# One load for each unit's weights: sixteen shared 4 KB buffers in a hybrid attention layer

## The chip, the cores and the metric

The kernel runs on one core of a Trainium2 chip. The metric is the device time of one execution in microseconds (us); the median of several runs is compared. A core has TensorE (matrix products, PE in the profile, its weight loads PEld), VectorE (DVE), ScalarE (ACT), GpSimd (POOL) and SyncE (SP); in this kernel SyncE issues every transfer (DMA), one after the other from one queue. Working memory is SBUF, 128 partitions wide; a "4 KB buffer" has 4 KB in each partition, 512 KB in all. Sums of products are built up in PSUM.

## The reference

One layer of a streaming encoder runs over a prompt of 2048 rows and a sample of 8 x 16 rows with caches of 512 past positions. The width is 1024. Cut to what matters:

```python
def adaln_modulate(x, c, norm_g, w_ada, b_ada):
    shift, scale, gate = jnp.split(c @ w_ada + b_ada, 3, axis=-1)
    h = rms_norm(x, norm_g) * (1.0 + scale[:, None, :]) + shift[:, None, :]
    return h, gate[:, None, :]

def project_inputs(h, w_in, pos):
    # columns of w_in: 4 x 512 (branch A), 4 x 512 (branch B), 2 x 1024 (gates)
    qa, ka, va, za, qb, kb, vb, zb, ga, gb = jnp.split(h @ w_in, idx, axis=-1)
    ...  # rope on qa, ka

def diff_attention(q, k, v, qpos, kpos, lam):          # branch A, 4 heads
    p = softmax(where(mask, q @ k.T / 8, -inf))         # two maps a head
    return (p[0] - lam * p[1]) @ v

def stick_breaking_attention(q, k, v, qpos, kpos):     # branch B, 8 heads
    z = q @ k.T / 8
    log_1m = where(mask, log_sigmoid(-z), 0.0)
    log_a = log_sigmoid(z) + cumsum(log_1m, reverse=True) - log_1m
    return where(mask, exp(log_a), 0.0) @ v

def merge_branches(oa, ob, za, zb, ga, gb, ...):
    ya = (rms_norm(oa, subln_g) * (1 - lam_init) * silu(za)) @ w_branch_a
    yb = (ob * silu(zb)) @ w_branch_b
    return (sigmoid(ga) * ya + sigmoid(gb) * yb) @ w_out

y = rms_norm(x + gate * merge_branches(...), final_g)   # also returns the new keys and values
```

All inputs are fp32.

## The kernel before, in words

Every product in fp32 is made of fp16 products. An operand is scaled by a power of two and split into a high and a low fp16 part, and three products (high x high, high x low, low x high) are summed. The power of two depends on the operand's sum of squares. So a weight is touched twice: first a *norm* (a sum of squares on ScalarE, `sum_squares`, whose unused output is the tile `junk`), then, when all chunks of the operand have been summed and the scale is known, a *cut* (`split`, L266: the high part on ScalarE or GpSimd in turn, the low part on VectorE).

The work is in eight *units*, `u` from 0 to 7. Unit u takes head group `h = u // 2` of branch A (`u` even) or of branch B (`u` odd). A unit's projection weights are 512 columns of `w_in` (query, key, value and z of that head group), in four chunks of 256 rows; a chunk is one 4 KB buffer, loaded by two DMAs of 256 KB (L298). Units 1 to 6 also project 256 columns of the gates (two chunks of 512 KB, L309), unit 7 projects 512 (four chunks).

Each unit goes over 17 row tiles, the sample tile first (`t == NT`), then the 16 prompt tiles. `project` (L388) multiplies a tile of activations `hg`, fetched from memory one tile ahead (`fetch_h`, L384, three buffers), with the unit's weights `U["w"]` (24 products of 128 x 512 at L409) and the gate weights `U["wg"]` (24 products at L476); `finish` scales the result, splits it and stores keys, values and z. `scores` forms the attention scores of a tile (L611 to L615) and turns the weights by a transposing DMA (`turn`, L552, tile `wt`); `pv` multiplies them with the values (L659 to L664) two steps later.

The main loop (L1170) goes over the 136 steps `(u, t)`. At each step it lays side by side the score work of that step, the values' work of two steps before, and a part of the list of projection pieces, which runs about five tiles ahead of the scores (`LEAD`). At the first step of unit u the pieces of `prepare_unit(u + 1)` are put on the list `back` and are handed out over the first nine steps (`W_READY`). When that list is empty, the step takes from `spare`, the norms of the output weights and of the caches (`norms`, L801): 80 loads of 512 KB, each followed by one sum of squares. The order on each engine's queue is then set by a scheduler with a timing model of its own; it keeps to the data dependencies, and an instruction that needs a buffer again waits for the last user of it.

`prepare_unit` (L286) makes the pieces: four norms, `bounds` (the scale), then two cuts, then the norms and cuts of the gates. The other two cuts (chunks 4 and 6) are returned apart and kept in `late`; `begin` (L824) runs them when the unit's own projection starts. A norm loads its chunk into one of two buffers of the pool `wst`, and a cut loads it again into one of them. Cut weights lie in 12 buffers of 2 KB (`wpr`, tile `wpair`; a unit needs 8) and, for the gates, in six of 4 KB (`gwp`, tile `gw`, opened when the startup is over). The spare norms use the two `wst` buffers too. Unit 0 is different: its raw chunks lie in a large tile of the startup (`keep`) and are loaded once.

The startup (the `p0` pool) computes the modulation, prepares unit 0, norms, modulates and transposes x, and starts the first projections. After the last projection all pools of `proj` are closed, and their place is taken by the pools for the branch weights, the merge and the output; the sample's attention over the caches runs there too.

Of the kernel before, what the change touches and what calls it, by code (L numbers as in the profile page):

```python
# [16 lines left out]
F32 = mybir.dt.float32  # L17
F16 = mybir.dt.float16
# [7 lines left out]
P = 128  # L26
D = 1024
KT = D // P
# [13 lines left out]
SC_BUFS = 6  # L42
V_LO, V_HI = 0.1, 1.0
W_READY = 9
W_BUFS = 12
WIDE_BUFS = 6
P0_AT = 2.0, 4.0, 6.0
K_BUFS = 6
V_BUFS = 23
G_BUFS = 6  # L50
S_TILES = 13
S_PERIOD = 6
H_AT = 2
# [58 lines left out]
def layer_kernel(ctx: ExitStack, tc: tile.TileContext, a: dict):  # L112
# [61 lines left out]
    unit = ctx.enter_context(tc.tile_pool(name="unit", bufs=2))  # L174
    proj = ctx.enter_context(ExitStack())
    c01 = ctx.enter_context(ExitStack())
    wpr = proj.enter_context(tc.tile_pool(name="wpr", bufs=W_BUFS, side="right", reuse_waits="tile"))
    wst = proj.enter_context(tc.tile_pool(name="wst", bufs=2, side="right", reuse_waits="tile"))
    kvp = c01.enter_context(tc.tile_pool(name="kvp", bufs=2))
    stg = c01.enter_context(tc.tile_pool(name="stg", bufs=2))  # L180

# [64 lines left out]
    def sum_squares(src, n, dst, width=1024):  # L246

        for i in range(0, n, width):
            junk = tiny.tile([P, width], F16, tag="junk", name="junk", bufs=1)
            w = min(width, n - i)  # L250
            S.activation(out=junk[:, 0:w], in_=src[:, i : i + w], func=AF.Square,  # L251
                         accum_out=dst[:, i // width : i // width + 1])
# [32 lines left out]

    def prepare_unit(u, keep=None):  # L286

        kept = {}
        h, kind = u // 2, u % 2
        U = dict(h=h, kind=kind, u=u)  # L290
        units[u] = U

        def chunk(k):
            if k in kept:
                return kept[k]
            st = wst.tile([P, 2, 4, P], F32, tag="wst", name="wst") if keep is None else keep[:, k // 2, :, :, :]
            for i in range(2):
                load(out=st[:, i, :, :], in_=w_in[:, k + i, :].rearrange("p (j n) -> p j n", n=512)[:, 4 * kind : 4 * kind + 4, h * P : (h + 1) * P])  # L298
            st = st.rearrange("p k j n -> p k (j n)")
            if keep is not None:  # L300
                kept[k] = st
            return st

        g0, gw = GATES[u]
        gk = 1024 // gw if gw else 0

        def gate_chunk(k):
            st = wst.tile([P, 2, 4, P], F32, tag="wst", name="wst").rearrange("p a j n -> p (a j n)").rearrange("p (k n) -> p k n", k=gk)
            load(out=st, in_=w_in[:, k : k + gk, 4096 + g0 : 4096 + g0 + gw])  # L309
            return st  # L310

        def gate_norm(k):
            if k == 0:
                U["gacc"] = unit.tile([P, 4], F32, tag="gacc", name="gacc")
            sum_squares(gate_chunk(k).rearrange("p k n -> p (k n)"), 1024, U["gacc"][:, k // gk : k // gk + 1])

        def gate_cut(k):
            if k == 0:
                U["sg"] = scales(total(add_up(U["gacc"], KT // gk)), unit, "sg")
                U["wg"] = []  # L320
            st = gate_chunk(k)
            w = gwp.tile([P, gk, 2, gw], F16, tag="gw", name="gw", bufs=G_BUFS)
            split(w[:, :, 0, :], w[:, :, 1, :], st, U["sg"][:, 0:1], S if k else G)
            U["wg"].append(w)

        def norm(k):
            if k == 0:
                U["acc"] = unit.tile([P, 4], F32, tag="wacc", name="wacc")
            sum_squares(chunk(k).rearrange("p k n -> p (k n)"), 1024, U["acc"][:, k // 2 : k // 2 + 1])

        def bounds():
            fsq = total(add_up(U["acc"], 4))
# [3 lines left out]
            U["w"] = []  # L336

        def cut(k):
            st = chunk(k)
            for i in range(2):  # L340
                w = wpr.tile([P, 2, 512], F16, tag="wpair", name="wpair")
                split(w[:, 0, :], w[:, 1, :], st[:, i, :], U["sw"][:, 0:1], S if i % 2 else G)
                U["w"].append(w)

        early = [lambda k=k: norm(k) for k in range(0, KT, 2)] + [bounds] + [lambda k=k: cut(k) for k in (0, 2)]
        if gw:
            early += [lambda k=k: gate_norm(k) for k in range(0, KT, gk)] + [lambda k=k: gate_cut(k) for k in range(0, KT, gk)]
        return early, [lambda k=k: cut(k) for k in (4, 6)]

    def finish_unit(u):  # L350

# [36 lines left out]
    def project(U, t):  # L388
# [80 lines left out]
        def gate_piece(n):  # L469

            if n == 0:
                box["g"] = bank("t")
            for j in range(per * n, per * n + per):
                hi, wi = ((0, 0), (0, 1), (1, 0))[j % 3]
                k = j // 3
                T.matmul(box["g"][:, 0:gw], box["h"][:, hi, k, :], U["wg"][k // per][:, k % per, wi, :], start=(j == 0), stop=(j == 3 * KT - 1))  # L476
            if per * n + per == 3 * KT:
                gt = gwp.tile([P, 512], F32, tag="gt", name="gt", bufs=2)
# [322 lines left out]
    def norms():  # L801

        srcs = [w[:, k, :] for w in (w_ba, w_bb) for k in range(4)] + [w_out[:, k, :] for k in range(KT)]
        srcs = [(src, wsums[:, i : i + 1]) for i, src in enumerate(srcs)]
        srcs += [(caches[name][:, i * 8 : i * 8 + 8, h * P : (h + 1) * P], csums[:, cache_column(name, h), i : i + 1])
                 for name in caches for h in range(4) for i in range(4)]

        def one(src, dst):
            st = wst.tile([P, 2, 4, P], F32, tag="wst", name="wst").rearrange("p k j n -> p (k j n)")
            load(out=st if len(src.shape) == 2 else st.rearrange("p (j n) -> p j n", n=P), in_=src)  # L810
            sum_squares(st, 1024, dst)

        return [lambda src=src, dst=dst: one(src, dst) for src, dst in srcs]
# [4 lines left out]
    jobs = []  # L818


    late = {}
    line = []

    def begin(u, t):  # L824
        if t == NT:
            for fn in late.pop(u, []):
                fn()
            finish_unit(u)

    def projection(m):  # L830
# [44 lines left out]
    with tc.tile_pool(name="p0", bufs=1) as p0:  # L875
# [57 lines left out]
        xs = {}  # L933
        for n in range(3):
            modulation(n)
        early, late0 = prepare_unit(0, hp_tile(F32).rearrange("p (a k j n) -> p a k j n", k=2, j=4, n=P))
        for fn in early[0:4]:
            fn()
        modulation(3)
        for fn in early[4:] + late0:  # L940
            fn()
        xs[4] = load_x(16, 1)
        xs[0] = load_x(0, 4)
# [404 lines left out]
```

## Time and profile before

| | |
|---|---|
| median of 3 runs | 2494.43 us (2491.0 to 2498.75) |
| the profiled execution | 2503.67 us, its span 2501.9 us |
| mean granted TensorE clock | 0.94 of full speed |
| PE busy | 2162.8 us (86%) |
| DVE busy | 1807.2 us (72%) |
| ACT busy | 1602.2 us (64%) |
| POOL busy | 833.8 us (33%) |
| bytes moved by DMA | 477.07 MB |
| weight loads into `wst` | 112 of 256 KB and 32 of 512 KB |

The profile is one execution. A group of instructions is named by line, engine, operation and tiles, written `out<-in` with buffer numbers left out. A line of the waits reads: engine, tile and line that stood idle, what ended that idle time, microseconds in all, times, the longest. The chain of waits is followed back from the last instruction, at each step to what released it; a piece of it is shown with its start, its length and its name. In the list of DMAs the last figure is the median time from issue to landing. Instructions that only wait or issue a DMA do not count as busy. The matmuls' ends are modelled, so a busy PE is not a PE at its peak.

### The profile page before, as it was taken

The page shows a single profiled execution, that of the slowest core. Times are in us where ns is not written, and L with a number is a line of the kernel's source. Part 1 is how long each engine was busy: PE and PEld are TensorE (multiplying, and loading weights), DVE is VectorE, ACT ScalarE, POOL GpSimd, SP SyncE. Part 2 cuts the span into 40 slices and gives each one's busy share as a digit, 9 for nine tenths or more (in the row PEclk, how much of TensorE's full clock was granted, in tenths as well). Part 3 has the DMA queues.
Part 4 walks back from the last instruction along what each step waited for, and adds up shares of the span by engine and source line. Part 5 has one row for each costly group of instructions (what it writes and reads, how often), then busy time and mean ns, then how long its engine had stood idle before and what let it go on. Part 6 is the DMA issues. An engine that isn't in the chain of part 4 may idle for free.

```text
span 2501.9 us, 45310 instructions
## 1 busy us (share of the span) xinstructions
PE 2162.8 (86%) x16366; PEld 1263.7 (51%) x16366; DVE 1807.2 (72%) x3769; ACT 1602.2 (64%) x3200; POOL 833.8 (33%) x671
## 2 busy tenths in 40 slices
PE   4779898889989988899989889999975789888887
PEld 2445465545655555556555555555543344444443
DVE  4868657876665788667668866656787888787855
ACT  4658667876766778666677866656775545454442
POOL 1822023352101335321124532102353465443422
PEclk7989999999999999999999999999986889899999
DMA  8779778996777899777688976656678998997521
GB/s 304 270 184 215 183 185 202 207 209 158 187 204 170 202 206 223 169 158 184 165 201 190 217 178 168 168 134 141 146 170 214 270 232 238 225 237 209 155 97 52
DMA packets 890994, 477.07 MB, mean 191 GB/s; under 512 B 540074, under 2 KB 842330, under 8 KB 890256
## 3 DMA queue, kind: packets, MB, share of 16 engines
q1 hardware_dynamic: 890768, 474.17, 76.2%
q8 instruction: 128, 2.10, 0.4%
q14 instruction: 98, 0.80, 0.1%
HBM read 272.94 MB, written 73.44 MB: 138 GB/s over the span
## 4 chain that ended last, share of the span: by engine, by line
PE 40%; DMA 19%; DVE 16%; ACT 9%; issue 8%; POOL 4%; SPq 3%; DVEq 0%; POOLq 0%; ACTq 0%
PE ps_mm L409 16%; PE ps_t L476 9%; DMA hg<-hT_d 5%; DMA wt<-sc_n 4%; DMA wst<-in_w_in_dram 3%; DVE sc_n L588 3%; PE ps_s L611 2%; PE ps_mm L1235 2%; PE ps_s L612 2%; ACT junk L251 2%; ACT sc_p L121 2%; PE ps_o L1274 2%; DVE sc_n L545 1%; ACT ps_s L121 1%; DVE o L1127 1%
## 5 line engine op out<-in xcount | busy, mean ns | idle before, releaser
L409 PE MATMUL ps_mm<-wpair,hg 128*128 128x512 f16 x3120 | 790.1, 388 | 58.5 <-DMA hg<-hT_d 54.8
L594 POOL TENSOR_TENSOR sc_p<-sc_p,sc_n 128x127 f32<-128x127 f32 (+7 forms) x192 | 313.5, 1637 | 808.5 <-DVE sc_n L588 790.8
L409 PEld LDWEIGHTS <-hg 128*128 128x128 f16 x3120 | 279.2, 99 | 330.7 <-DMA hg<-hT_d 67.2
L476 PE MATMUL ps_t<-gw,hg 128*128 128x256 f16 (+1 forms) x2856 | 393.8, 292 | 2.5 <-DVE qst L504 1.7
L476 PEld LDWEIGHTS <-hg 128*128 128x128 f16 x2856 | 278.7, 99 | 96.3 <-DVE qst L504 2.5
L588 DVE TENSOR_TENSOR_SCAN sc_n<-ps_s,sc_n,zero_t 128x512 f32<-128x512 f32 x192 | 245.6, 1279 | 69.2 <-ACT ps_s L121 64.5
L611 PE MATMUL ps_s<-k,qst 128*128 128x512 f16 (+3 forms) x640 | 228.1, 358 | 52.4 <-DVE sc_n L588 41.3
L545 DVE TENSOR_TENSOR sc_n<-sc_p,sc_n 128x128 f16<-128x128 f32 (+7 forms) x192 | 234.5, 1227 | 36.8 <-ACT sc_n L544 36.2
L121 ACT ACTIVATE sc_p<-ps_s,usc 128x512 f32<-128x512 f32 (+3 forms) x320 | 204.8, 640 | 48.7 <-PE ps_s L612 24.0
L612 PE MATMUL ps_s<-k,qst 128*128 128x512 f16 (+3 forms) x640 | 227.6, 358 | 0.0
L1235 PE MATMUL ps_mm<-wb,uT 128*128 128x512 f16 x816 | 200.0, 398 | 21.4 <-DVE o L1133 13.0
L121 ACT ACTIVATE ps_s<-ps_s,usc 128x512 f32<-128x512 f32 (+3 forms) x328 | 199.8, 609 | 0.0
L1274 PE MATMUL ps_o<-wo,yT 128*128 128x512 f16 x816 | 193.8, 392 | 6.7 <-POOL wo L271 4.8
L663 PE MATMUL ps_o<-v,wt 128*128 128x128 f16 x1088 | 162.3, 228 | 42.4 <-DMA wt<-sc_n 42.4
L544 ACT CAST sc_n<-sc_p 128x128 f16<-128x128 f32 (+7 forms) x192 | 154.8, 813 | 44.3 <-POOL sc_p L594 43.4
L442 POOL TENSOR_TENSOR rot<-pr,rope 128x256 f32<-128x256 f32 x68 | 60.5, 890 | 358.7 <-ACT pr L423 314.6
L251 ACT ACTIVATE junk<-wst 128x1024 f16<-128x1024 f32 x124 | 131.4, 1059 | 71.8 <-DMA wst<-in_w_in_dram 23.9
L530 DVE TENSOR_SCALAR_CACHE_REDUCE sc_p<-ps_s,usc 128x512 f32<-128x512 f32 (+3 forms) x160 | 106.5, 666 | 77.7 <-PE ps_s L612 48.3
L663 PEld LDWEIGHTS <-wt 128*128 128x128 f16 x1088 | 106.1, 103 | 95.3 <-DMA wt<-sc_n 49.8
L664 PE MATMUL ps_o<-v,wt 128*128 128x64 f16 x1088 | 150.6, 200 | 0.0
L530 DVE TENSOR_SCALAR_CACHE_REDUCE sc_n<-ps_s,usc 128x512 f32<-128x512 f32 (+3 forms) x160 | 106.5, 666 | 49.3 <-PE ps_s L615 31.3
L1235 PEld LDWEIGHTS <-uT 128*128 128x128 f16 x816 | 81.1, 102 | 119.2 <-issue 39.7
(295 smaller groups left out, 4343.9 us busy)
## 6 DMA issues: line engine op xcount, KB each, us to landing
hg<-hT_d SPq DMA_DIRECT2D x130, 512.0 KB, 4.7
wst<-in_w_in_dram SPq DMA_DIRECT2D x112, 256.0 KB, 4.0
g<-g_d SPq DMA_DIRECT2D x34, 512.0 KB, 6.4
wst<-in_w_in_dram SPq DMA_DIRECT2D x32, 512.0 KB, 4.4
out_dram<-pr SPq DMA_DIRECT2D x204, 64.0 KB, 2.3
g_d<-gt SPq DMA_DIRECT2D x102, 128.0 KB, 3.6
wide<-in_w_ada_dram SPq DMA_DIRECT2D x12, 1024.0 KB, 10.8
z_d<-pr SPq DMA_DIRECT2D x136, 64.0 KB, 2.4
```

What stands on the lines that cost most here:

```text
L121: i = S.activation(**kw)
L409: T.matmul(box["p"], box["h"][:, hi, k, :], U["w"][k][:, wi, :], start=(n == 0), stop=(n == 3 * KT - 1))
L476: T.matmul(box["g"][:, 0:gw], box["h"][:, hi, k, :], U["wg"][k // per][:, k % per, wi, :], start=(j == 0), stop=(j == 3 * KT - 1))
L530: V.tensor_scalar(out=dst[:, lo : lo + n], in0=p[:, 0:n], scalar1=sc_pos, scalar2=None, op0=ALU.mult, op1=ALU.max, accum_out=job["mx"][:, ...
L545: V.tensor_tensor(out=lo, in0=src, in1=hi, op=ALU.subtract)
L588: V.tensor_tensor_scan(out=dst[:, lo : lo + n][:, ::-1], data0=src[:, 0:n][:, ::-1], data1=zero_t[:, 0:1].to_broadcast([P, n]), initial=fi ...
L594: G.tensor_tensor(out=p[:, 0:m], in0=p[:, 0:m], in1=n[:, 1 : m + 1], op=ALU.mult)
L611: T.matmul(p[:, 0:n], qst[:, c, :], kk[:, c, 0:n], start=True, stop=False)
L612: T.matmul(p[:, 0:n], qst[:, 2 + c, :], kk[:, c, 0:n], start=False, stop=not diag)
L663: T.matmul(po[:, c * P : (c + 1) * P], wt[:, wj, :], vt[:, c, :, :], start=first, stop=False)
L1235: T.matmul(pb, st["u"][:, ui * 8 + br * 4 + k, :], wb[:, br, wi, k, c], start=(n == 0), stop=(n == 11))
L1274: T.matmul(po, st["y"][:, yi * 8 + k, :], wo[:, wi, k, c], start=(n == 0), stop=(n == 3 * KT - 1))
```

## The change

All weight buffers of the units become sixteen buffers of 4 KB on one list, `free`: eight (`wa`) open from the start, eight (`wb`) open when the startup is over. A norm takes a buffer off the list and loads the chunk there; it stays until its cut. A cut takes another buffer off the list for its result (a 4 KB chunk in fp32 becomes 4 KB of high and low parts) and puts the raw buffer back at the end. The unit's result buffers are kept in `U["bufs"]` and go back on the list when the projection of the next unit begins. All four cuts of a unit are among the early pieces, and `late` is gone. The scale of the gates is a piece of its own (`bounds_g`). The spare norms take the first buffer of the list and put it at the end at once, so that they go round all free buffers.

```diff
-W_BUFS = 12
-G_BUFS = 6
...
-    wpr = proj.enter_context(tc.tile_pool(name="wpr", bufs=W_BUFS, side="right", reuse_waits="tile"))
-    wst = proj.enter_context(tc.tile_pool(name="wst", bufs=2, side="right", reuse_waits="tile"))
+    free = []
+
+    def open_buffers(name, n):
+        pool = proj.enter_context(tc.tile_pool(name=name, bufs=1, side="right", reuse_waits="tile"))
+        free.extend(pool.tile([P, 1024], F32, name=f"{name}{i}") for i in range(n))
+
+    open_buffers("wa", 8)
...
     def prepare_unit(u, keep=None):
...
-        def chunk(k):
-            if k in kept:
-                return kept[k]
-            st = wst.tile([P, 2, 4, P], F32, tag="wst", name="wst") if keep is None else keep[:, k // 2, :, :, :]
-            for i in range(2):
-                load(out=st[:, i, :, :], in_=w_in[:, k + i, :]...)
...
+        def fetch(name, k):
+            raw[name, k] = b = free.pop(0) if keep is None else keep[:, k // 2, :]
+            if name == "w":
+                st = b.rearrange("p (k j n) -> p k j n", k=2, n=P)
+                for i in range(2):
+                    load(out=st[:, i, :, :], in_=w_in[:, k + i, :]...)
+            else:
+                load(out=b.rearrange("p (k n) -> p k n", k=gk), in_=w_in[:, k : k + gk, 4096 + g0 : 4096 + g0 + gw])
+
+        def norm(name, k, i):
             if k == 0:
...
+            fetch(name, k)
+            sum_squares(raw[name, k], 1024, U[name + "acc"][:, i : i + 1])
...
+        def split_to(name, k):
+
+            b = free.pop(0)
+            U["bufs"].append(b)
+            if keep is None:
+                free.append(raw[name, k])
+            return raw[name, k], b.bitcast(F16)
 
         def cut(k):
-            st = chunk(k)
+            st, w = split_to("w", k)
             for i in range(2):
-                w = wpr.tile([P, 2, 512], F16, tag="wpair", name="wpair")
-                split(w[:, 0, :], w[:, 1, :], st[:, i, :], U["sw"][:, 0:1], S if i % 2 else G)
-                U["w"].append(w)
-
-        early = [lambda k=k: norm(k) for k in range(0, KT, 2)] + [bounds] + [lambda k=k: cut(k) for k in (0, 2)]
+                x = w.rearrange("p (i f n) -> p i f n", i=2, f=2)[:, i, :, :]
+                split(x[:, 0, :], x[:, 1, :], st[:, i * 512 : (i + 1) * 512], U["sw"][:, 0:1], S if i % 2 else G)
+                U["w"].append(x)
...
+        pieces = [lambda k=k: norm("w", k, k // 2) for k in range(0, KT, 2)] + [bounds] + [lambda k=k: cut(k) for k in range(0, KT, 2)]
         if gw:
-            early += [lambda k=k: gate_norm(k) for k in range(0, KT, gk)] + [lambda k=k: gate_cut(k) for k in range(0, KT, gk)]
-        return early, [lambda k=k: cut(k) for k in (4, 6)]
+            pieces += [lambda k=k: norm("g", k, k // gk) for k in range(0, KT, gk)] + [bounds_g] + [lambda k=k: gate_cut(k) for k in range(0, KT, gk)]
+        return pieces
...
         def one(src, dst):
-            st = wst.tile([P, 2, 4, P], F32, tag="wst", name="wst").rearrange("p k j n -> p (k j n)")
+            st = free.pop(0)
+            free.append(st)
...
     def begin(u, t):
         if t == NT:
-            for fn in late.pop(u, []):
-                fn()
+            if u > 0:
+                free.extend(units[u - 1]["bufs"])
             finish_unit(u)
...
-    gwp = proj.enter_context(tc.tile_pool(name="gwp", bufs=1, side="right", reuse_waits="tile"))
+    gtp = proj.enter_context(tc.tile_pool(name="gtp", bufs=1, side="right", reuse_waits="tile"))
+    open_buffers("wb", 8)
...
             if t == NT and u < 7:
-                early, late[u + 1] = prepare_unit(u + 1)
-                back += early
+                back += prepare_unit(u + 1)
```

More of the change, by code (lines that the diff above doesn't have):

```diff
@@ L286, in prepare_unit @@
     def prepare_unit(u, keep=None):
-        kept = {}
         h, kind = u // 2, u % 2
-        U = dict(h=h, kind=kind, u=u)
+        U = dict(h=h, kind=kind, u=u, w=[], wg=[], bufs=[])
         units[u] = U
-        def chunk(k):
-            if k in kept:
-                return kept[k]
-            st = wst.tile([P, 2, 4, P], F32, tag="wst", name="wst") if keep is None else keep[:, k // 2, :, :, :]
-            for i in range(2):
[L298 to L302, printed above, removed]
+        raw = {}
@@ L304, in prepare_unit @@
         g0, gw = GATES[u]
         gk = 1024 // gw if gw else 0
[L307 to L312, printed above, removed]
-            if k == 0:
-                U["gacc"] = unit.tile([P, 4], F32, tag="gacc", name="gacc")
-            sum_squares(gate_chunk(k).rearrange("p k n -> p (k n)"), 1024, U["gacc"][:, k // gk : k // gk + 1])
@@ L317, in gate_cut @@
[L317 to L329, printed above, removed]
+        def fetch(name, k):
[3 more added lines that the diff above has]
+                for i in range(2):
+                    load(out=st[:, i, :, :], in_=w_in[:, k + i, :].rearrange("p (j n) -> p j n", n=512)[:, 4 * kind : 4 * kind + 4, h * P : (h + 1) * P])
+            else:
+                load(out=b.rearrange("p (k n) -> p k n", k=gk), in_=w_in[:, k : k + gk, 4096 + g0 : 4096 + g0 + gw])
@@ L331, in bounds @@
+        def norm(name, k, i):
+            if k == 0:
+                U[name + "acc"] = unit.tile([P, 4], F32, tag=name + "acc", name=name + "acc")
+            fetch(name, k)
+            sum_squares(raw[name, k], 1024, U[name + "acc"][:, i : i + 1])
         def bounds():
-            fsq = total(add_up(U["acc"], 4))
+            fsq = total(add_up(U["wacc"], 4))
             U["sw"] = scales(fsq, unit, "sw")
@@ L335, in bounds, with bounds_g, gate_cut @@
             V.tensor_copy(out=U["fsq"], in_=fsq)
-            U["w"] = []
+        def bounds_g():
+            U["sg"] = scales(total(add_up(U["gacc"], KT // gk)), unit, "sg")
+        def split_to(name, k):
[4 more added lines that the diff above has]
+            return raw[name, k], b.bitcast(F16)
         def cut(k):
-            st = chunk(k)
+            st, w = split_to("w", k)
             for i in range(2):
-                w = wpr.tile([P, 2, 512], F16, tag="wpair", name="wpair")
-                split(w[:, 0, :], w[:, 1, :], st[:, i, :], U["sw"][:, 0:1], S if i % 2 else G)
-                U["w"].append(w)
-        early = [lambda k=k: norm(k) for k in range(0, KT, 2)] + [bounds] + [lambda k=k: cut(k) for k in (0, 2)]
+                x = w.rearrange("p (i f n) -> p i f n", i=2, f=2)[:, i, :, :]
+                split(x[:, 0, :], x[:, 1, :], st[:, i * 512 : (i + 1) * 512], U["sw"][:, 0:1], S if i % 2 else G)
+                U["w"].append(x)
+        def gate_cut(k):
+            st, w = split_to("g", k)
+            w = w.rearrange("p (k f n) -> p k f n", k=gk, f=2)
+            split(w[:, :, 0, :], w[:, :, 1, :], st.rearrange("p (k n) -> p k n", k=gk), U["sg"][:, 0:1], S if k else G)
+            U["wg"].append(w)
+        pieces = [lambda k=k: norm("w", k, k // 2) for k in range(0, KT, 2)] + [bounds] + [lambda k=k: cut(k) for k in range(0, KT, 2)]
         if gw:
-            early += [lambda k=k: gate_norm(k) for k in range(0, KT, gk)] + [lambda k=k: gate_cut(k) for k in range(0, KT, gk)]
-        return early, [lambda k=k: cut(k) for k in (4, 6)]
+            pieces += [lambda k=k: norm("g", k, k // gk) for k in range(0, KT, gk)] + [bounds_g] + [lambda k=k: gate_cut(k) for k in range(0, KT, gk)]
+        return pieces
     def finish_unit(u):
@@ L477, in gate_piece @@
             if per * n + per == 3 * KT:
-                gt = gwp.tile([P, 512], F32, tag="gt", name="gt", bufs=2)
+                gt = gtp.tile([P, 512], F32, tag="gt", name="gt", bufs=2)
                 S.activation(out=gt[:, 0:gw], in_=box["g"][:, 0:gw], func=AF.Identity, scale=sc[:, 6:7])
@@ L818, in layer_kernel @@
     jobs = []
-    late = {}
     line = []
@@ L935, in layer_kernel @@
             modulation(n)
-        early, late0 = prepare_unit(0, hp_tile(F32).rearrange("p (a k j n) -> p a k j n", k=2, j=4, n=P))
+        early = prepare_unit(0, hp_tile(F32).rearrange("p (a n) -> p a n", n=1024))
         for fn in early[0:4]:
@@ L939, in layer_kernel @@
         modulation(3)
-        for fn in early[4:] + late0:
+        for fn in early[4:]:
             fn()
```

## The prediction

> **What bounds the kernel now.** I read the page first, then the granted clock and busy time by windows, then the chain of waits and the waits by engine between 250 and 1850 us. In that stretch each unit's projections, scores and values run with the preparation of the next unit beside them; the startup lies before it and the branches and output after it.
>
> ```profile
> span 2501.9 us, 45310 instructions
> PE 2162.8 (86%) x16366; PEld 1263.7 (51%) x16366; DVE 1807.2 (72%) x3769; ACT 1602.2 (64%) x3200; POOL 833.8 (33%) x671
> DMA packets 890994, 477.07 MB, mean 191 GB/s; under 512 B 540074, under 2 KB 842330, under 8 KB 890256
> q1 hardware_dynamic: 890768, 474.17, 76.2%
> ```
>
> ```profile
> 0.00:150.00 150.00, 89.43 (x587) 48.41 (x588) 103.19 (x281) 79.11 (x156) 69.37 (x77) 0.85 0.79 273
> 250.00:1850.00 1600.00, 1452.59 (x11197) 894.64 (x11198) 1122.94 (x2258) 1132.29 (x2361) 448.68 (x367) 0.97 0.78 181
> 1850.00:2502.00 652.00, 523.28 (x3914) 268.06 (x3912) 508.90 (x1026) 313.55 (x502) 285.56 (x194) 0.87 0.72 194
> ```
>
> In a window's row the busy times of PE, weight loads, VectorE, ScalarE and GpSimd follow the length; the last three figures are granted clock, DMA share and GB/s. In the middle stretch TensorE is busy for 1452.6 of 1600 us at a clock of 0.97, so 147 us are all that it can win there by waiting less. What ended its waits, in the waits of PE over that stretch:
>
> ```profile
> PE ps_mm L409 <- DMA hg<-hT_d: 49.2, 34, 3.9
> PE ps_s L611 <- DVE sc_n L588: 26.3, 26, 2.4
> PE ps_o L663 <- DMA wt<-sc_n: 26.2, 20, 3.1
> PE ps_o L659 <- DMA wt<-sc_n: 20.7, 14, 3.2
> ```
>
> The activations (hg) and the turned attention weights (wt) come late, 96.1 us together; a projection weight is not in the list. The weights appear one step back, as waits of ScalarE and GpSimd, which work in order and have other work queued behind:
>
> ```profile
> ACT junk L251 <- DMA wst<-in_w_in_dram: 21.5, 13, 3.4
> ACT wpair L269 <- DMA wst<-in_w_in_dram: 19.6, 10, 3.8
> ACT junk L251 <- DMA wst<-in_cache_a_k_dram: 13.0, 9, 3.2
> ACT junk L251 <- DMA wst<-in_cache_a_v_dram: 12.5, 8, 4.9
> ACT junk L251 <- DMA wst<-in_cache_b_k_dram: 11.5, 5, 3.8
> ACT junk L251 <- DMA wst<-in_w_out_dram: 4.7, 3, 2.9
> ACT junk L251 <- DMA wst<-in_cache_b_v_dram: 2.0, 2, 1.6
> ```
>
> That is 84.8 us in 50 waits, 1.7 us each: ScalarE stands at a sum of squares or a split while one of two `wst` buffers is still being filled. The chain of waits says that such loads do reach the end. Of the chain in the middle stretch, by line:
>
> ```profile
> by line: PE ps_mm L409 20.4%; PE ps_t L476 14.3%; DMA hg<-hT_d 7.0%; issue 6.4%; DMA wt<-sc_n 5.0%; DMA wst<-in_w_in_dram 4.1%; PE ps_s L611 3.3%; PE ps_s L612 3.1%; DVE sc_n L588 3.0%; ACT sc_p L121 2.7%; ACT junk L251 2.3%; ACT ps_s L121
> ...
> 405.11 6.84 DMA wst<-in_cache_a_k_dram
> ...
> 1302.96 6.13 DMA wst<-in_cache_b_v_dram
> ```
>
> Weight loads hold 4.1% of 1600, 65.6 us, 16 pieces among the longest listed; loads of the caches, for their norms, stand there with 13 pieces from the first to the last shown. A piece in the chain is a whole load; what goes with it is only the time to whatever came second.
>
> **The change part by part.**
>
> *Loads removed.* Units 1 to 7 load each weight once instead of twice. Eight 256 KB loads per unit go, 56 in all; of the 512 KB gate loads go two for each of units 1 to 6 and four for unit 7, 16 in all:
>
> ```profile
> hg<-hT_d SPq DMA_DIRECT2D x130, 512.0 KB, 4.7
> wst<-in_w_in_dram SPq DMA_DIRECT2D x112, 256.0 KB, 4.0
> wst<-in_w_in_dram SPq DMA_DIRECT2D x32, 512.0 KB, 4.4
> wide<-in_x_prompt_dram SPq DMA_DIRECT2D x16, 512.0 KB, 10.0
> ```
>
> Half of 112 and half of 32: the built program of the changed kernel has these 72 copies fewer, all on SyncE's queue, so the change does what it says. In bytes 56 x 0.262 + 16 x 0.524 = 23.1 MB of 477.07, 4.8%. The DMA engines are not the bound over the stretch (share 0.78), but hg and wt stand in their queue. If those waits of TensorE shrink as the traffic, 96.1 x 0.048 = 5 us go. From both sides: 0 where the waits come from the issue and not from the drain; 15 where they shrink three times as fast, because the removed loads fall together with the transposes. I take 5.
>
> *The late splits.* Chunks 4 and 6 of a unit used to be loaded again and split at the unit's first projection. Now all four are split early. What TensorE itself waited for them:
>
> ```profile
> who waited for it (us, times):
> ...
>   POOL wpair L271: 39.1, 8
> ...
>   PE ps_mm L409: 3.2, 3
> ```
>
> These are waits for `wst` in the middle stretch, and I take the 3 us of PE. The splits themselves are only moved, from the projection's begin into the unit before, among its first nine score steps. Their durations are in the rows of `wst`:
>
> ```profile
> L274 DVE SCALAR_TENSOR_TENSOR wpair<-wst,sw,wpair x56: 719/741/1574, 128.5 to 1595.7; 128x512 f16<-128x512 f32 x56
> L269 ACT ACTIVATE wpair<-wst,sw x28: 705/722/784, 127.5 to 1592.2; 128x512 f16<-128x512 f32 x28
> L271 POOL TENSOR_SCALAR wpair<-wst,sw x28: 686/692/1408, 128.6 to 1591.5; 128x512 f16<-128x512 f32 x28
> ```
>
> Two chunks a unit are four VectorE instructions (3.0 us), two on ScalarE (1.4) and two on GpSimd (1.4), for seven units. No instruction is added on these engines. VectorE is idle for 30% of the stretch and ScalarE for 29%, which hides the move at either place; without that cover it costs 3.0 us a unit, 21 in all, and as it leaves another place free, 21 could also be won. I take nothing.
>
> *More buffers ahead of ScalarE.* This is the term that decides. Before, two buffers took every load. After, a unit keeps four (six with gates, eight for unit 7) and the rest of the sixteen pass round, ten of them while a unit is being prepared. The built order shows what the scheduler makes of it: between a weight load and its sum of squares stand 326 matmuls in the median instead of 48, between load and split 675 instead of 97, and for the caches 56 to 223 by kind instead of 34 to 125. With 11197 matmuls in 1600 us (the window's row) one stands for 0.143 us, so 48 are 7 us, little more than the 4.0 that a load takes to land, and 326 are 47 us: ScalarE's 84.8 us of waits on `wst` should nearly all go. How much reaches the end? The chain goes through 29 such loads (16 and 13). ScalarE waited 1.7 us at each on average, 49 us. Where the wait goes, next in line is the sum's own queue: TensorE's own work, or hg and wt, which already ended most of TensorE's idle time. I take half, 25 us. The ends: 0, if a second releaser stands right behind every time, and 65.6 + 65.6 = 131 us, if the whole pieces of the chain go (the 13 cache pieces listed add up to 65.6 as well).
>
> *GpSimd* waited 39.1 us for the same loads in 8 waits; it is busy for 449 of 1600 us, and the wait lies inside idle time. Nothing is taken for it.
>
> *Startup.* Unit 1's weights now find four buffers free at once, so eight loads of 256 KB are issued before and among the first loads of x instead of four: 1.05 MB more at 273 GB/s (window 0 to 150) is 3.8 us, partly hidden by the modulation; later in startup ten reloads of weights and gates go. I take +2, from -3 to +4.
>
> *After 1850 us* nothing is added or removed; the pools that open there lie where the weights lay, and wait for the last projection as before.
>
> *Waits added.* A load into a buffer that a former unit's weights held waits for that unit's last projection matmul, on SyncE's in-order queue, with hg, wt and the stores behind it. In the built order the buffer is mostly free when the load's turn comes, as the scheduler places a load when it becomes so; the same queue waited for ScalarE's sums in the same way before, some microseconds a line:
>
> ```profile
> SPq L810 <- ACT junk L251: 12.0, 11, 2.5
> SPq L298 <- ACT junk L251: 9.2, 7, 3.3
> ```
>
> I take zero for the exchange, with its rival below.
>
> Sum: -5 - 3 - 25 + 2 = -31 us. The profiled execution took 2503.67 us, 1.8 us more than its span, and becomes 2472.7. It lies 9.2 us above the median of the three runs, so on the median's scale 2494.4 - 31 = 2463. The scheduler writes a new order for every engine, which I cannot price from a row; the three runs spread over 7.8 us, and I add that much on either side.
>
> **The rivals.**
>
> *Bursts ahead of hg and wt: slower.* When unit u begins, the six buffers of unit u-1 are freed at one moment, and the built order puts eight loads (2.1 MB) into about 50 matmuls, 7 us, on the queue that also carries hg and wt. The trace shows what a 512 KB load costs behind such a crowd: the loads of x, issued twelve in a row, take 10.0 us to land, hg 4.7, so 5.3 us more. TensorE waits for hg already, 34 times in the stretch. With six units, two hg or wt loads delayed by the burst at a unit's start, and again two by the run of cache loads behind it, 24 x 5.3 = 127 us would be added; half of it hidden leaves 64, less the 31: 2494 + 33 = 2527. It decides from six such delays on (6 x 5.3 = 32). For it: SyncE's queue is shared and in order. Against it: the loads before came in fours as well, the whole traffic is less, and in the built order the number of matmuls between issue and use of hg and wt has not fallen (median 53 against 43 for hg, 41 against 39 for wt). The Trainium skill (DMA: Bandwidth & Descriptors, Queues, rings and completion order) says that SyncE has one ring on each DMA engine and descriptors are consumed in ring order, so by that rule the 2.1 MB ahead of hg are paid in full, 11.6 us at the stretch's 181 GB/s and 70 us over six units. The landing times of x agree that such waits exist; no row here shows one of 11.6 us.
>
> *The cover was complete: no change.* hg and wt end 96 of TensorE's 147 idle microseconds, weights only 3. If ScalarE's waits were spent while TensorE waited for those anyway, only the 3 and the 5 are left, less the startup's 2: 2488, within what a measurement of this kernel can tell from no change (0.3%, 7.5 us). For it: ScalarE is busy for 1132 of 1600 us and can catch up. Against it: the chain's 4.1%.
>
> *Three times the gain.* Most of the chain's 131 us of loads go whole, as nothing stands close behind: -100, 2394. For it: the loads come in runs, and what ScalarE does after them is in the chain as well (L251 2.3%). Against it: TensorE has only 147 us of idle time in all.
>
> **How the numbers follow.** The forecast has 0.50; its own range, with the half taken between a fifth and all of 49 us and the spread of the runs, is 2430 to 2485. Bursts 0.22, no change 0.14, the great gain 0.14. The range must leave out no more than 0.2: it goes down to 2420, a third of the way into the great gain, and up to 2508, where the bursts cost about 45 us and the savings are more than eaten. Faster by over 0.3%: 0.50 + 0.14, 0.64. Within: 0.14. Slower: 0.22.
>
> **What would show it.** In the changed kernel's profile: 72 fewer copies and about 454 MB; ScalarE's waits for weight and cache loads under 15 us in the middle stretch; these loads gone from the chain; PE's busy share there above 0.92. hg and wt landing in 4.7 us or less speaks for the forecast; landing in 6 us and more, with PE's waits for them over 130 us, for the bursts. If ScalarE's waits are gone and the stretch is as long as before, the cover was complete. I am wrong if TensorE's waits grow where the loads come early, or if the time moves before 250 or after 1850 us.

## The result, and the profile after

The changed kernel takes 2438.9 us in the median of four runs (2434.9 to 2445.6), the kernel before 2496.6 in four: 57.7 us or 2.25% faster, ratio 0.9775 (95% interval 0.9752 to 0.9798). The prediction was 2463, 31 us faster. The profiled execution took 2436.4 us.

The page after, its totals:

```profile
span 2434.6 us, 45193 instructions
PE 2138.5 (88%) x16366; PEld 1252.6 (51%) x16366; DVE 1811.3 (74%) x3769; ACT 1601.5 (66%) x3200; POOL 840.5 (35%) x671
DMA packets 854000, 453.98 MB, mean 186 GB/s; under 512 B 538922, under 2 KB 806362, under 8 KB 853264
q1 hardware_dynamic: 853776, 451.09, 74.3%
hg<-hT_d SPq DMA_DIRECT2D x130, 512.0 KB, 4.6
```

The compute engines run the same instructions, 23.1 MB less is moved, and hg lands in 4.6 us (median) instead of 4.7. To find the place I took the moments at which both traces stand at the same piece of work. The 13th load of hg is issued at 231.0 us before and at 231.3 after, so the startup gave nothing. The last weights of attention are turned at 1910 and at 1852: the 58 us are between these two, in the stretch of the units. The windows, columns as before, first of the kernel before and then of the changed one:

```profile
0.00:231.00 231.00, 169.17 (x1109) 90.55 (x1109) 156.52 (x442) 139.12 (x299) 94.07 (x105) 0.90 0.81 243
231.00:1910.00 1679.00, 1500.48 (x11557) 923.51 (x11557) 1198.90 (x2368) 1190.49 (x2461) 487.47 (x389) 0.96 0.78 182
1910.00:2502.00 592.00, 493.10 (x3700) 249.67 (x3700) 451.79 (x960) 272.62 (x441) 252.30 (x177) 0.90 0.71 194
```

```profile
0.00:231.00 231.00, 173.43 (x1106) 93.94 (x1107) 161.01 (x445) 137.18 (x295) 95.91 (x107) 0.85 0.77 242
231.00:1852.00 1621.00, 1474.66 (x11570) 911.74 (x11568) 1201.40 (x2366) 1189.46 (x2462) 494.23 (x387) 0.98 0.75 175
1852.00:2435.00 583.00, 490.41 (x3692) 246.90 (x3692) 448.85 (x960) 274.89 (x445) 250.38 (x177) 0.92 0.72 198
```

In the stretch TensorE's idle time falls from 178.5 to 146.3 us, 32 of the 58. The other 26 are busy time: about as many matmuls, 1474.7 us instead of 1500.5, at a granted clock of 0.98 instead of 0.96. The 9 us of the last window are in a part that the change does not touch. The profiled execution of before was 7 us slower than its median and the one after 2.5 faster, and in the twelve traces below this part takes between 579 and 591 us without being touched, so I don't count them; the 58 are one pair of executions and uncertain by as much.

What ended TensorE's waits in the stretch, first before (the rows of hg and wt), then after:

```profile
PE ps_mm L409 <- DMA hg<-hT_d: 49.2, 34, 3.9
PE ps_o L663 <- DMA wt<-sc_n: 39.9, 24, 7.7
PE ps_o L659 <- DMA wt<-sc_n: 21.0, 15, 3.2
```

```profile
PE ps_mm L409 <- DMA hg<-hT_d: 42.1, 30, 3.2
PE ps_o L663 <- DMA wt<-sc_n: 39.9, 31, 7.3
PE ps_s L611 <- DVE sc_n L588: 32.2, 31, 3.1
PE ps_o L659 <- DMA wt<-sc_n: 21.4, 19, 3.6
```

hg and wt still lead, with 103.4 us against 110.1; the burst of loads did not make them late. (The trace has the landing of only 14 of the 118 loads of hg in the stretch; none of these took more than 5.5 us. TensorE's longest wait for hg fell from 3.9 to 3.2 us.) And ScalarE's waits for the loads, the first six of nine rows (the smaller three are 1.9, 1.2 and 0.3):

```profile
ACT junk L255 <- DMA wa<-in_cache_a_k_dram: 9.4, 6, 2.0
ACT junk L255 <- DMA wb<-in_cache_a_v_dram: 6.5, 3, 3.5
ACT junk L255 <- DMA wb<-in_w_in_dram: 6.3, 3, 4.0
ACT junk L255 <- DMA wb<-in_cache_b_v_dram: 5.7, 4, 1.9
ACT junk L255 <- DMA wb<-in_cache_b_k_dram: 3.8, 3, 2.2
ACT junk L255 <- DMA wa<-in_w_out_dram: 3.5, 2, 3.2
```

That is 38.6 us of the 84.8. Waits for `w_in` are nearly gone (6.6 us instead of 41.1), but those for the norms of the caches fall only from 39.0 to 28.5 us, though sixteen buffers are shared where there were two. The chain of waits of this trace, followed back from the end, breaks off before it reaches the stretch, so whether the loads have left the chain can't be read.

### The profile page after: what moved, and what is told of

It is laid out like the page before. It is cut to its first block, busy times and chain, and to the rows that moved or that the text cites. A ratio compares the mean times of both kernels' runs of the same rounds, so it can differ in the third digit from the quotient of the medians.

```text
span 2434.6 us, 45193 instructions
## 1 busy us (share of the span) xinstructions
PE 2138.5 (88%) x16366; PEld 1252.6 (51%) x16366; DVE 1811.3 (74%) x3769; ACT 1601.5 (66%) x3200; POOL 840.5 (35%) x671
## 5 line engine op out<-in xcount | busy, mean ns | idle before, releaser
L594 POOL TENSOR_TENSOR sc_p<-sc_p,sc_n 128x127 f32<-128x127 f32 (+7 forms) x192 | 320.0, 1669 | 765.4 <-DVE sc_n L588 734.4
L409 PEld LDWEIGHTS <-hg 128*128 128x128 f16 x3120 | 276.1, 99 | 312.4 <-DMA hg<-hT_d 61.0
L409 PE MATMUL ps_mm<-wa,hg 128*128 128x512 f16 x1590 | 400.3, 384 | 30.2 <-DMA hg<-hT_d 30.1
L409 PE MATMUL ps_mm<-wb,hg 128*128 128x512 f16 x1530 | 388.7, 383 | 19.1 <-DMA hg<-hT_d 19.1
L476 PEld LDWEIGHTS <-hg 128*128 128x128 f16 x2856 | 276.0, 98 | 92.8 <-DVE qst L504 4.3
L545 DVE TENSOR_TENSOR sc_n<-sc_p,sc_n 128x128 f16<-128x128 f32 (+7 forms) x192 | 227.7, 1191 | 27.7 <-ACT sc_n L544 27.3
L476 PE MATMUL ps_t<-wb,hg 128*128 128x256 f16 (+1 forms) x1734 | 244.5, 293 | 0.7 <-DVE qst L504 0.6
L476 PE MATMUL ps_t<-wa,hg 128*128 128x256 f16 (+1 forms) x1122 | 148.4, 282 | 1.0 <-DVE qst L504 1.0
```

The costliest lines, as they stand in the source:

```text
L409: T.matmul(box["p"], box["h"][:, hi, k, :], U["w"][k][:, wi, :], start=(n == 0), stop=(n == 3 * KT - 1))
L545: V.tensor_tensor(out=lo, in0=src, in1=hi, op=ALU.subtract)
L594: G.tensor_tensor(out=p[:, 0:m], in0=p[:, 0:m], in1=n[:, 1 : m + 1], op=ALU.mult)
```

## The experiments

Theory A was the prediction's: depth ahead of ScalarE. B: the traffic. C: the late cuts. D: SyncE waiting for buffers. Two more came out of the first runs. E: each instruction on SyncE's queue has a price. F: the new order that the scheduler makes of everything is the cause. All ratios are to the kernel before, measured beside it on the same chip; 0.001 is 2.5 us. Variants of the changed kernel are compared through their ratios, so a difference between two of them is uncertain by about 0.0035, or 9 us.

| kernel | ratio | interval |
|---|---|---|
| the changed kernel | 0.9775 | 0.9752 to 0.9798 |
| before, four staging buffers | 0.9909 | 0.9881 to 0.9937 |
| before, all cuts early | 0.9881 | 0.9844 to 0.9918 |
| changed, each second load back and waited for | 0.9880 | 0.9851 to 0.9909 |
| changed, second loads into free buffers, not read | 0.9940 | 0.9920 to 0.9959 |
| changed, full copies to scratch | 0.9871 | 0.9846 to 0.9896 |
| changed, 72 small copies | 0.9856 | 0.9829 to 0.9883 |
| changed, 144 small copies | 0.9926 | 0.9909 to 0.9943 |
| changed, 72 small copies from GpSimd | 0.9778 | 0.9759 to 0.9796 |
| changed, norms in two buffers | 0.9819 | 0.9793 to 0.9845 |
| changed, fifteen buffers | 0.9798 | 0.9766 to 0.9830 |
| changed, fifteen, four hg buffers | 0.9822 | 0.9806 to 0.9839 |
| changed, rotation table from GpSimd | 0.9847 | 0.9830 to 0.9864 |

**Depth alone, in the kernel before.**

```diff
-            st = wst.tile([P, 2, 4, P], F32, tag="wst", name="wst")   # two buffers
+            st = ring.pop(0); ring.append(st)                         # four, in turn
```

> The kernel before, with four staging buffers taken in turn instead of two (the two new ones open when the startup is over); every second load and the late cuts stay. If the depth ahead of ScalarE makes the gain (theory A), half of it or more is here: 20 to 40 us faster than before, and ScalarE's waits for weight and cache loads fall from 85 us to 45 or less. If the 23 MB of traffic makes it (theory B), or the late cuts (theory C): within 8 us of before.

23 us faster. ScalarE's waits for these loads fell from 86 to 47 us, nearly as far as in the changed kernel (39), and yet 33 us of the gain are missing. Depth is worth something, and ScalarE's waits are not the measure of it.

**Early cuts alone, in the kernel before.**

```diff
-        early = ... + [lambda k=k: cut(k) for k in (0, 2)]
+        early = ... + [lambda k=k: cut(k) for k in range(0, KT, 2)]     # sixteen pair buffers
...
-        return early, [lambda k=k: cut(k) for k in (4, 6)]
+        return early, []
```

> The kernel before, with sixteen 2 KB buffers for cut weights instead of twelve, so that all four chunks of a unit are cut early and nothing is loaded at a unit's begin; two staging buffers and every second load stay. Theory C (the late cuts stood in the way at each unit's begin): 20 us or more faster than before. Theory A: 3 us, and at most 10, since TensorE waited 3 us for late weights. Theory B: none.

30 us faster, against my 3. ScalarE waits for loads as long as before (83 us). TensorE's wait for hg, 49.2 us before over the stretch, fell:

```profile
PE ps_mm L410 <- DMA hg<-hT_d: 32.8, 20, 4.2
```

So the price of the late cuts isn't TensorE's wait for a weight (3 us). That they hurt through what stood with them on the queues at a unit's begin is my reading and not shown: the scheduler made a new order here too, TensorE's waits for wt rose by 5 us while those for hg fell, and no run tells which queue it was.

**The traffic put back.**

```diff
             if keep is None:
+                g = free.pop(0); free.append(g)
+                fill(g, name, k)              # the chunk again; nothing reads it
                 free.append(raw[name, k])
```

> The changed kernel with the 72 loads put back as traffic alone: at each cut the chunk is loaded again into the next free buffer, and nothing reads it. Theory B: 25 us or more slower than the changed kernel, so over 2465 us. Theory A: 0 to 8 us slower, as nobody waits for these loads and the DMA engines have a quarter of their time free. If SyncE's in-order queue is what the loads cost, it shows here as well, as longer waits of TensorE for hg and wt.

2479.6 us: 41 us of the gain lost, though nobody reads these loads. ScalarE's waits were 40.1 us, about the same as in the changed kernel; their three longest rows:

```profile
ACT junk L255 <- DMA wb<-in_w_in_dram: 9.0, 4, 4.6
ACT junk L255 <- DMA wa<-in_cache_b_k_dram: 8.4, 4, 4.0
ACT junk L255 <- DMA wb<-in_cache_a_v_dram: 5.5, 2, 4.1
```

Here theory A falls as the main term. B seemed to win, but these loads also take buffers, which SyncE must wait for, so two of the next runs part bytes, buffers and instructions.

**The norms in two buffers.**

```diff
-            st = free.pop(0)
+            st = free.pop(-2)
             free.append(st)
```

> The changed kernel with the 80 norm loads of output weights and caches going round the last two entries of the free list, so that they have two buffers as before, while the units' weights keep theirs. If the norms' depth is half of theory A: 15 to 25 us slower than the changed kernel, and ScalarE's waits for cache loads back at 40 us. If the gain is in the units' weights alone: within 8 us of the changed kernel.

About 11 us slower than the changed kernel, between the two expectations, and the intervals overlap a little. ScalarE's waits stayed at 37 us. The depth of the norms is a small part at most.

**The same bytes, no buffer; and a sixteenth of the bytes.** After the split of each chunk its piece of `w_in` is copied to scratch in HBM, all 128 rows or 8 of them.

```diff
+            ghost("w", k, last)     # load(out=scratch[0:n, ...], in_=w_in[0:n, ...]), n = 128 or 8
```

> The changed kernel with the 72 removed transfers put back as traffic that touches no buffer of the kernel: the same pieces of w_in, 256 or 512 KB, are copied into scratch in HBM that nothing reads, each placed after the split of its chunk. If the bytes and packets on the shared DMA engines are the price (theory B): 25 to 45 us slower than the changed kernel, as with the loads into the list's buffers, ratio to before 0.988 or more. If those were slow because they took buffers and made SyncE wait (theory D): within 10 us of the changed kernel.

> The same with 8 of 128 rows copied: as many transfers on SyncE's queue, a sixteenth of the bytes and packets. Theory B: within 10 us of the changed kernel. If the issue of 128 further instructions on SyncE's in-order queue is the price: as slow as with the full copies.

(The instructions added are 72, not the 128 that the second text names.) Full copies cost 24 us, small ones 20: no difference that these intervals can tell, though the DMA share is 0.80 against 0.75. First the full, then the small copies:

```profile
231.00:1888.00 1657.00, 1491.06 (x11580) 920.08 (x11578) 1196.90 (x2373) 1190.67 (x2468) 484.07 (x386) 0.97 0.80 184
```

```profile
231.00:1882.00 1651.00, 1495.51 (x11558) 921.10 (x11555) 1197.81 (x2369) 1189.93 (x2464) 487.49 (x385) 0.96 0.75 172
```

The bytes cost 4 us, too little to be told from nothing; 72 instructions on SyncE cost more. B falls as the main cause. D explains at most the 17 us by which the unread loads into buffers were slower than full copies to scratch, and the traces don't bear even that out: between the 13th load of hg and the last turned weights the unread loads take 1654 us and the full copies 1660, so what the unread loads lose beyond the full copies they lose before and after that.

The small copies don't make TensorE wait for what SyncE brings. Its waits for hg fell, those for hg and wt together from 103.4 to 78.3 us:

```profile
PE ps_mm L423 <- DMA hg<-hT_d: 20.1, 14, 3.6
```

The stretch is 30 us longer than in the changed kernel, and 21 of them are busy time of TensorE at a lower granted clock.

**Twice as many, and from another engine.**

```diff
-    copies = [load(...) ...]                       # nc.sync, 8 rows
+    copies = [load(...) ... for r in (0, 8)]       # twice as many
...
+    copies = [G.dma_start(...) ...]                # or 72 from GpSimd
```

> The changed kernel with each of the 72 small copies (8 rows, to scratch in HBM, read by nothing) issued twice, for different rows: 144 more instructions on SyncE's queue than the changed kernel, about an eighth of the bytes of the removed loads. 72 of them cost about 20 us (ratio to before 0.986 against 0.978). If the price is SyncE's time, 0.28 us for each instruction (theory E): 35 to 45 us slower than the changed kernel, ratio 0.993 or more. If the 20 us came from the new order that the scheduler made (theory F): anywhere within 10 us of the 72 copies.

> The changed kernel with the 72 small copies issued by GpSimd, which is idle for two thirds of the time, instead of SyncE. Theory E: at least half of their 20 us comes back, ratio to before 0.982 or less, and PE's waits fall to those of the changed kernel. If any copy costs as much, whoever issues it: ratio 0.985 or more.

The second 72 cost 17 us after the first 20: 0.26 us for each of 144 on average. From GpSimd the same 72 cost nothing that shows (0.9778 against 0.9775), and TensorE's waits in all are 143.0 us in the stretch, against 144.7 in the changed kernel and 150.0 with the copies from SyncE. That is what E forecast, but for a ratio of 0.993 that 0.9926 just misses. F alone is unlikely, though a new order is in every one of these runs: all five kernels with more transfers on SyncE's queue than the changed one have ratios of 0.9856 to 0.9940, all six without, the changed one included, 0.9775 to 0.9847. The two groups nearly touch, through the rotation table below, but they don't mix. So the price goes with the place on SyncE's queue. Summed over the stretch of each trace, SyncE's own DMA instructions occupy it for 1021 of 1621 us in the changed kernel, 1097 of 1651 with 72 small copies, 1148 of 1667 with 144, and 1026 of 1631 with the copies on GpSimd. It is occupied for 63 to 69% of the time and so not full; that the price comes by delaying what stands behind is argued, and which delay reaches TensorE is not shown. Nor is it shown that SyncE's time is the price and not the DMA queue behind it, since copies from GpSimd go through another queue (q0 instead of q1 on the page); against the latter speaks that hg and wt land in 4.5 and 4.2 us with the full copies and in 4.4 and 4.1 without, in the few landings that the traces have. One such instruction occupies SyncE and GpSimd for about as long (a group's least, median and greatest ns; the small copies of unit 3, from SyncE and from GpSimd):

```profile
L338 SPq DMA_DIRECT2D ghost3w<-in_w_in_dram x8: 631/641/709, 555.5 to 563.3; - x8
```

```profile
L338 POOL DMA_DIRECT2D ghost3w<-in_w_in_dram x8: 548/548/607, 549.9 to 553.8; - x8
```

The Trainium skill (Trainium Kernel Development and Optimization, Key Constraints) says that DMAs issued from several engines run on the same DMA engines and that spreading them only saves the sequencer's issue time. The runs agree, and here what was saved was worth 20 us.

**Each second load back and waited for.**

```diff
             if keep is None:
+                fill(raw[name, k], name, k)   # the same chunk again, before its split
                 free.append(raw[name, k])
```

> The changed kernel with the second load put back where it was waited for: each cut loads its chunk again into the raw buffer before it splits it. Theory A and B: all but 10 us of the gain is lost, ratio to before 0.995 or more. If only the waiting counts and the traffic nothing, it is slower than with the copies that nobody reads, by 20 us or more; if the traffic alone counts, as slow as those.

2474.0 us: a ratio of 0.988, 26 us over the changed kernel, as much as copies that nobody waits for. The waiting for a second load costs nothing that shows; its place on SyncE's queue does. About 30 us of the gain remain without saving a single load.

**Fifteen buffers.**

```diff
-    open_buffers("wb", 8)
+    open_buffers("wb", 7)
```

> The changed kernel with fifteen buffers, which still suffice for unit 7. The scheduler makes a new order of everything, so this shows what a new order alone is worth: within 8 us of the changed kernel if the depth is ample. If every buffer counts: 10 us slower or more.

6 us slower, with intervals that overlap. It is one sample of what a new order brings: differences under 10 us between these kernels should not be explained. It doesn't bound a new order's worth, as the next section shows.

**Two tries at less on SyncE's path.**

```diff
-                load(out=box["r"], in_=a["shapes"][...])
+                G.dma_start(out=box["r"], in_=a["shapes"][...])
...
-    hst = ... bufs=3 ...
+    hst = ... bufs=4 ...                       # and fifteen weight buffers
```

> The changed kernel with the 68 loads of the rotation table (48 KB each, 0.42 us of issue on SyncE) issued by GpSimd, which uses the table. Theory E: SyncE has 51 instructions fewer in the stretch of the projections, so 10 to 15 us faster than the changed kernel, ratio to before 0.973 or less. If SyncE's time is not the price: within 5 us of the changed kernel, or slower where GpSimd's own order suffers.

> The changed kernel with fifteen weight buffers and a fourth buffer for activations (hg). TensorE waits 42 us for hg in the changed kernel, and SyncE stands 75 us at the load of hg until TensorE has freed a buffer. If the in-order queue is blocked there for the transfers behind it: 15 us or more faster than fifteen buffers alone (ratio 0.980), and SyncE's wait for TensorE at that line under 30 us. If hg's load is late for another reason: within 8 us of fifteen buffers alone.

Both missed. With the rotation table issued by GpSimd, SyncE has 68 instructions fewer, and the kernel is 18 us slower than the changed one. This speaks against E, at least against a fixed price for each instruction. GpSimd's busy time in the stretch is 522 instead of 494 us; but the 72 copies on GpSimd had 520 and cost nothing, so that is not the reason by itself. GpSimd's own products use the table, but its trace has no wait for it in the stretch. The cause stays open, and a worse order is among the candidates. With the fourth hg buffer TensorE's wait for hg fell to 11.9 us (23.9 with fifteen buffers alone), and the wait for VectorE's scan rose to 51.2 (40.8):

```profile
PE ps_s L611 <- DVE sc_n L588: 51.2, 50, 3.5
PE ps_o L663 <- DMA wt<-sc_n: 42.7, 26, 5.7
PE ps_o L659 <- DMA wt<-sc_n: 13.1, 8, 3.3
PE ps_mm L409 <- DMA hg<-hT_d: 11.9, 7, 2.6
```

The time did not follow (0.9822 against 0.9798 for fifteen buffers), and SyncE's longest row of waits for TensorE at the load of hg stayed, at 67.6 against 64.0 us. TensorE's waits change their name when one of them is mended. None of the kernels tried beats the changed one. As it is the fastest of the six kernels without added transfers on SyncE's queue, each in an order of its own, some of its gain may be a lucky order.

## Why the prediction was right, and where not

The direction, the place (between 250 and 1850 us) and the range were right; the sum was half of what came. Two of its terms were far too small, and the range held because it left room for all of the 49 us that the third gave to ScalarE's waits, which turned out not to be the measure. That the time fell inside is in part luck.

- *Loads removed, 5 us:* about 26, from 0.9880 with each second load to 0.9775 without. I priced bytes on the DMA engines, and those cost next to nothing. 20 of the 26 come back with 72 instructions on SyncE's queue that move a sixteenth of the bytes (each occupies SyncE for 0.63 us or more, a removed load for 0.38 to 0.49 in the median, so the two prices need not be equal). The step that failed is the choice of the resource: the rows of SyncE's waits were before me, and I set them to zero as an exchange, without counting what 72 fewer instructions leave free on the one queue that hg, wt and all stores share.
- *The late splits, 3 us:* 30 when done alone in the kernel before. Here I took the wait of the one engine that reads the weights for the price of the step. What the price is made of stays open.
- *Depth ahead of ScalarE, 25 us:* 23 alone. The figure fits by luck, the reason does not: ScalarE's waits fell nearly as far with four staging buffers, and with the unread loads, as in the changed kernel, at ratios of 0.9909 and 0.9940. Nor did they nearly all go, as the distances in the built order had led me to expect: 38.6 of 84.8 us stayed, most of them for the caches.
- The terms don't add: 23 and 30 alone are 53, together (with the loads still doubled) 30. Then 26 for the second loads, in all 56. Each of these figures holds a new order as well.
- *Startup, +2:* 0.3. *GpSimd, 0:* its waits for the loads are gone, and no run prices them.
- *The order's lottery, 8 us:* 6 in the run with fifteen buffers; the 18 of the rotation table, if they are that, would be more than twice the allowance.

The rivals. The bursts did not come: hg lands in 4.6 us where the landing is known, and TensorE's waits for hg and wt fell by 7 us in the same stretch. By the ring order that the Trainium skill (DMA: Bandwidth & Descriptors, Queues, rings and completion order) describes, the 2.1 MB ahead of hg would have cost up to 70 us; no such wait shows, as TensorE's longest wait for hg is 3.2 us. "The cover was complete" is out. The great gain, 100 us, did not come either; 57.7 lies between it and the forecast, nearer to the forecast.

Of the signs that I named, 72 copies and 454 MB came as written. ScalarE's waits under 15 us (38.6 came) and a busy share above 0.92 did not: the share of PE is 0.910 from 250 to 1850 us, as its matmuls became shorter together with its waits. Whether the loads are gone from the chain can't be read.

## What to carry to other kernels

Where one queue issues all transfers in order, count its instructions as a resource of its own: here a transfer that nobody waits for cost a quarter of a microsecond on average, with a sixteenth of the bytes nearly as much as with all of them, and the same transfer from an idle engine nothing. Test it for each transfer, as moving the rotation table's loads made the kernel slower. A wait that the profile shows beside a load tells where an engine stood, not what the step is worth: the late cuts showed 3 us and were worth 30. And when one wait is taken away and another grows by as much, look for what bounds them both before mending the next.

## What the runs showed of the hardware

In the two traces nearly half of the gain came through TensorE's clock. In the stretch of the units the granted clock went from 0.96 to 0.98, and about as many matmuls were busy for 26 us less, while idle time fell by 32. The record of the granted clock says how: it is either full or half, and in the stretch it stands at half 26 times before, for 136 us in all, and 13 times after, for 80 us. Those 56 us at half speed are worth up to 28 us of full speed, which is about the busy time that went. The Trainium skill (TensorE: Matmul & The Clock Gate, Part 1: The HAM clock gate) says that the clock drops to half after a window without enough activity and comes back after a busy one. The record agrees: in both traces each drop in the stretch comes after 3.4 us in which TensorE was busy for less than half of the time, and most last 3.4 us. With fewer such gaps less is lost, so that here a microsecond of waiting saved was worth almost two. It also bears on the 72 small copies from SyncE: with them the clock stands at half for 126 us, nearly as long as before the change.
